# A third of the modulation's dot products, moved from VectorE to GpSimd and ScalarE

## The chip, the cores and the metric

The kernel runs on one core of one Trainium2 chip. The time is the device time of one execution, in microseconds (us). TensorE (PE in the profile) multiplies matrices, VectorE (DVE), ScalarE (ACT) and GpSimd (POOL) work on elements, and SyncE (SP) issues most of the DMAs. Each engine runs its own instructions in order and waits for the others at semaphores.

## The reference, cut to what matters

Two blocks of two layers each run one after the other on 512 rows of 1024 values. Each layer of the first block begins with a modulation, a vector of 6 x 1024 values that shifts, scales and gates the rows of that layer:

```python
c_act = jax.nn.silu(c)                               # 1 x 1024
for layer in range(DEPTH):                           # 2 layers
    mod = c_act @ ada_w[layer] + ada_b[layer]        # 1024 x 6144 weights
    shift1, scale1, gate1, shift2, scale2, gate2 = jnp.split(mod, 6, axis=-1)
    h = modulate(rmsnorm(x, norm1_w[layer]), shift1, scale1)
    ...                                              # layer 0: pooling and attention; layer 1: a state-space mixer
    x = x + gate1[:, None, :] * mix
    h2 = modulate(rmsnorm(x, norm2_w[layer]), shift2, scale2)
    ffn = hier_moe(h2, ...)                          # a router picks 2 of 32 experts for each row
    x = x + gate2[:, None, :] * ffn
```

## The kernel before, in words

Rows lie transposed: a tile holds 128 of the 1024 features on its partitions and the 512 rows along its columns. Every large product is made in three matmuls of split values: a weight tile of 128x1024 is loaded into a stage buffer (`stage`, L286), ScalarE copies its high half (`split`, L278, tile whi), VectorE subtracts to get the low half (L279, tile wlo), and TensorE runs 24 matmuls over it (`mm3`, L304). `proj` does this for one tile of outputs; each call is one step of the program. The stage pool has four buffers, and SP issues the loads in order.

The modulation is not worth a matmul. Its 48 columns per layer (128 values each) are dot products of a transposed weight tile of 128x1024 with the activated vector, which is repeated on all partitions (`cact`, tile row in the profile). One `matvec` loads a tile through the same four stage buffers and lets VectorE multiply and sum it in one instruction (`dot`, L340):

```python
self.nc.vector.scalar_tensor_tensor(t if out is None else out, t, 1.0, vec, op0=OP.mult, op1=OP.mult, accum_out=acc)
```

The first 16 columns of layer 0 are needed at once and are computed ahead of all else (`shift_scale`). The others are pieces of work (`ada_cols`) that `weave` puts into the steps at a rate: 3 to each step of layer 0's mixer, then 1.38 to each step of the state-space mixer. The first list holds columns 16 to 47 of layer 0, then 16 of the second block's modulation, then columns 0 to 15 of layer 1; columns 16 to 47 of layer 1 follow in the state-space mixer. After each eighth column VectorE adds the biases (L407). A scheduler fixes the final order of each engine's instructions from the program.

Around this work stand, in order: layer 0's mixer (projections q, k and u, attention heads in pieces, eight tiles of output weights mix_out), the router of the first mixture of experts (its mask ob is waited for at L839), the experts, the sum of squares (sq on ScalarE, sqa on GpSimd and VectorE in turn, L353 and L355), the normalisation factor rstd as exponential of a logarithm on ScalarE (L367, L368), normalised rows (hhi, L391), and the state-space mixer (weights ssmA), in which GpSimd prepares the tiles aL (L1196). GpSimd's other work in the mixer are running sums for pooling (L612, L613).

Of the kernel before, what the change touches and what calls it, by code (L numbers as in the profile page):

```python
# [15 lines left out]
AF = mybir.ActivationFunctionType  # L16
OP = mybir.AluOpType
# [236 lines left out]
class K:  # L254
# [77 lines left out]
        while q and q[0]:  # L332
            q[0].pop(0)()

    def matvec(self, src, vec, acc):

        self.dot(self.stage(src), vec, acc)

    def dot(self, t, vec, acc, out=None):
        self.nc.vector.scalar_tensor_tensor(t if out is None else out, t, 1.0, vec, op0=OP.mult, op1=OP.mult, accum_out=acc)  # L340
# [58 lines left out]
    def ada_cols(self, l, rng):  # L399

        def one(j):
            def f():
                self.matvec(self.I["adaT"][l, j], self.cact, self.mod[l][:, j:j + 1])
                if j % 8 == 7:
                    a, _ = self.at[f"ada_b{l}"]
                    m = self.mod[l][:, j - 7:j + 1]
                    self.nc.vector.tensor_tensor(m, m, self.cols[:, a + j - 7:a + j + 1], op=OP.add)  # L407
            return f
        return [one(j) for j in rng]
# [1796 lines left out]
```

## Time and profile before

| what | us |
|---|---|
| three executions | 3007.97, 3021.48, 3018.7 |
| their median | 3018.7 |
| profiled execution | 3013.05 |
| its span | 3011.3 |
| TensorE busy | 2827.6 |
| VectorE busy | 1902.1 |
| ScalarE busy | 1254.9 |
| GpSimd busy | 512.4 |

The span goes from the first to the last instruction; what lies around it makes up the profiled execution's time. A row of the profile names the line, engine and operation, the tiles written and read, the count, and the idle time of the engine ahead of it with what ended it.

### The profile page before, as it was taken

How to read it: one execution, taken by the hardware profiler on the slowest of the kernel's cores; microseconds unless marked ns; L12 is line 12 of the kernel's file. 1: busy time of each engine (PE TensorE's matmuls, PEld its weight loads, DVE VectorE, ACT ScalarE, POOL GpSimd, SP SyncE). 2: the span in 40 equal slices, each digit the busy share in tenths (PEclk: the TensorE clock that was granted, in tenths of full speed). 3: DMA queues.
4: the chain of work that ended last, by engine and by line, in shares of the span. 5: the costliest groups of instructions: out<-in, count | busy, mean ns of one | idle time of the engine just before them, and what ended most of it. 6: DMA issues, size and time to landing. Idle time of an engine off the chain costs nothing.

```text
span 3011.3 us, 38668 instructions
## 1 busy us (share of the span) xinstructions
PE 2827.6 (94%) x14382; PEld 2157.5 (72%) x14382; DVE 1902.1 (63%) x3188; ACT 1254.9 (42%) x1989; POOL 512.4 (17%) x451
## 2 busy tenths in 40 slices
PE   7998998799999999887899999999999999999998
PEld 5566855677777786566787677777888767777886
DVE  7787423688889862247789555459547955444444
ACT  3444322455535452246543443343434344333333
POOL 0111321132403232112300100012120000002112
PEclk9999999899999999999999999999999999999999
DMA  8668997555542289974732222237444222222332
GB/s 291 221 224 298 343 412 288 176 176 155 161 143 63 89 309 385 357 262 150 224 111 70 60 77 77 92 113 225 146 139 126 77 63 67 84 91 80 96 91 78
DMA packets 163856, 503.76 MB, mean 167 GB/s; under 512 B 22864, under 2 KB 45008, under 8 KB 151376
## 3 DMA queue, kind: packets, MB, share of 16 engines
q1 hardware_dynamic: 149520, 467.67, 46.5%
q0 software_dynamic: 14144, 33.58, 3.1%
q8 instruction: 114, 1.87, 0.2%
q14 instruction: 78, 0.64, 0.1%
HBM read 472.98 MB, written 46.01 MB: 172 GB/s over the span
## 4 chain that ended last, share of the span: by engine, by line
PE 45%; DVE 4%; issue 1%; ACT 1%; DMA 1%; POOL 0%; DVEq 0%; ACTq 0%; POOLq 0%
PE mm L304 36%; PE po L1492 1%; PE pp L1489 1%; DVE wlo L279 1%; PE po L1415 1%; PE st L1404 1%; PE as L1705 1%; DVE stage L340 1%; PE as L1712 1%; DMA stage<-in_modT_dram 1%; PE pv L1602 0%; PE pv L1601 0%; DVE junk L340 0%; PE po L1426 0%; PE pv L1600 0%
## 5 line engine op out<-in xcount | busy, mean ns | idle before, releaser
L304 PE MATMUL mm<-hhi,whi 128*128 128x512 f32 (+1 forms) x2488 | 932.8, 375 | 11.9 <-ACT hhi L391 4.3
L304 PE MATMUL mm<-hhi,wlo 128*128 128x512 f32 (+1 forms) x2488 | 912.7, 367 | 16.6 <-DVE wlo L279 16.3
L304 PE MATMUL mm<-hlo,whi 128*128 128x512 f32 (+1 forms) x2488 | 909.8, 366 | 0.7 <-POOL hlo L396 0.7
L278 ACT ACTIVATE whi<-stage 128x1024 fp32r<-128x1024 f32 (+2 forms) x477 | 461.5, 968 | 872.2 <-PE mm L304 604.9
L279 DVE TENSOR_TENSOR wlo<-stage,whi 128x1024 fp32r<-128x1024 f32 (+2 forms) x477 | 546.0, 1146 | 425.5 <-issue 193.9
L304 PEld LDWEIGHTS mm<-hhi,whi 128*128 128x128 f32 x2488 | 474.6, 191 | 113.3 <-issue 27.5
L304 PEld LDWEIGHTS mm<-hhi,wlo 128*128 128x128 f32 x2488 | 474.2, 191 | 106.0 <-DVE wlo L279 24.3
L304 PEld LDWEIGHTS mm<-hlo,whi 128*128 128x128 f32 x2488 | 474.6, 191 | 84.9 <-issue 17.6
L340 DVE SCALAR_TENSOR_TENSOR stage<-stage,row 128x1024 f32<-128x1024 f32 x160 | 210.8, 1327 | 24.3 <-DMA stage<-in_adaT_dram 16.6
L1581 POOL TENSOR_TENSOR merged<-sig,merged 128x512 f32<-128x512 f32 x48 | 83.7, 1745 | 559.3 <-DVE sig L1580 550.0
L1617 DVE SCALAR_TENSOR_TENSOR cv<-cfu,cols,cv 128x512 f32<-128x512 f32 x240 | 172.3, 767 | 1.3
L304 PE MATMUL mm<-brh,whi 128*128 128x512 f32 (+1 forms) x384 | 143.0, 373 | 14.0 <-DVE merged L1578 5.8
L304 PE MATMUL mm<-brh,wlo 128*128 128x512 f32 (+1 forms) x384 | 142.3, 374 | 12.7 <-DVE wlo L279 12.4
L304 PE MATMUL mm<-brl,whi 128*128 128x512 f32 (+1 forms) x384 | 139.8, 364 | 0.1
L917 PE MATMUL pa<-w,xc 128*64 128x256 f32 x1056 | 132.4, 391 | 4.1 <-DMA w<-in_w_dram 4.0
L917 PEld LDWEIGHTS pa<-w,xc 128*64 128x64 f32 x1056 | 77.5, 139 | 48.1 <-issue 7.4
L304 PEld LDWEIGHTS mm<-brh,whi 128*128 128x128 f32 x384 | 75.4, 196 | 29.6 <-DVE merged L1578 6.6
L304 PEld LDWEIGHTS mm<-brh,wlo 128*128 128x128 f32 x384 | 75.2, 197 | 27.8 <-DVE wlo L279 16.1
L353 POOL TENSOR_TENSOR sqa<-sq,sqa 128x512 f32<-128x512 f32 (+1 forms) x44 | 58.5, 1329 | 188.8 <-ACT sq L355 183.5
L1356 ACT ACTIVATE att<-as,stat 128x512 f32<-128x512 f32 (+2 forms) x80 | 54.7, 686 | 70.7 <-DVE stat L1467 67.2
L304 PEld LDWEIGHTS mm<-brl,whi 128*128 128x128 f32 x384 | 75.7, 197 | 9.6 <-issue 0.5
L1196 POOL TENSOR_TENSOR aL<-cmt,aah 128x512 fp32r<-128x512 f32 x32 | 51.1, 1598 | 171.1 <-PE pe L1198 143.4
(476 smaller groups left out, 4273.5 us busy)
## 6 DMA issues: line engine op xcount, KB each, us to landing
stage<-in_winA_dram SPq DMA_DIRECT2D x252, 512.0 KB, 3.5
w<-in_w_dram SPq DMA_DIRECT2D x96, 1024.0 KB, 11.7
stage<-in_adaT_dram SPq DMA_DIRECT2D x96, 512.0 KB, 4.5
stage<-in_modT_dram SPq DMA_DIRECT2D x64, 512.0 KB, 3.8
stage<-in_ssmA_dram SPq DMA_DIRECT2D x49, 512.0 KB, 3.5
stage<-in_wbrA_dram SPq DMA_DIRECT2D x96, 256.0 KB, 2.7
stage<-in_woutA_dram SPq DMA_DIRECT2D x24, 512.0 KB, 3.6
dpc<-out SPq DMA_DIRECT2D x41, 256.0 KB, 4.9
```

The costliest lines, as they stand in the source:

```text
L278: self.nc.scalar.activation(hi, src, AF.Copy)
L279: self.nc.vector.tensor_tensor(lo, src, hi.bitcast(FT), op=OP.subtract)
L304: nc.tensor.matmul(ps[:, po:po + n], w[:, k * P:(k + 1) * P], h[:, so:so + n], start=(k == first and w is hi and h is hh), stop=(k == last ...
L340: self.nc.vector.scalar_tensor_tensor(t if out is None else out, t, 1.0, vec, op0=OP.mult, op1=OP.mult, accum_out=acc)
L353: (engine or nc.gpsimd).tensor_tensor(self.sq_acc, self.sq_last, self.sq_acc, op=OP.add)
L917: nc.tensor.matmul(pa[t * C:(t + 1) * C, :256], x[:, k, t * C:(t + 1) * C], w[:, c:c + 256], start=(k == 0), stop=(k == KT - 1))
L1196: nc.gpsimd.tensor_tensor(aL, self.cm("le")[:, None, :].to_broadcast([P, 4, P]), part[:, c, hsl, None].bitcast(FT).to_broadcast([P, 4, P]) ...
L1356: self.nc.scalar.activation(out, in_, func, **kw)
L1404: nc.tensor.matmul(q["ps"][:, i, :T], kT[:, j * P:(j + 1) * P], qT, start=True, stop=True)
L1415: nc.tensor.matmul(q["po"][:, :T], v[j][:, h * P:(h + 1) * P], q[j], start=(j == 0), stop=(j == nt - 1 and cross is None))
L1581: nc.gpsimd.tensor_tensor(merged[f], sg, merged[f], op=OP.add)
L1617: nc.vector.scalar_tensor_tensor(c, u[:, t:t + T], self.col(f"cfw{l}_{t}", i), c, op0=OP.mult, op1=OP.add)
```

## The change

`matvec` gets a flag. With it, GpSimd multiplies the stage tile by the vector in place, and ScalarE copies the product in place and sums it into the column. `ada_cols` sets the flag for columns whose number is a multiple of 3. `ada_cols` makes columns 16 to 47 of layer 0 and all 48 of layer 1, so these are 10 columns of layer 0 (18, 21, ..., 45) and 16 of layer 1 (0, 3, ..., 45), 26 in all; 6 of layer 1's fall into layer 0's mixer. The second block's modulation and `shift_scale` call `matvec` and `dot` without the flag.

```diff
-    def matvec(self, src, vec, acc):
-
-        self.dot(self.stage(src), vec, acc)
+    def matvec(self, src, vec, acc, shared=False):
+
+        t = self.stage(src)
+        if shared:
+            self.nc.gpsimd.tensor_tensor(t, t, vec, op=OP.mult)
+            self.nc.scalar.activation(t, t, AF.Copy, accum_out=acc)
+        else:
+            self.dot(t, vec, acc)
...
-                self.matvec(self.I["adaT"][l, j], self.cact, self.mod[l][:, j:j + 1])
+                self.matvec(self.I["adaT"][l, j], self.cact, self.mod[l][:, j:j + 1], j % 3 == 0)
```

The scheduler then sets other orders on every engine. Lines behind `matvec` move down by 5.

ScalarE at the seam between the first mixture of experts and the state-space mixer; sq are squares of the rows, ms their mean, rstd the normalisation factor. Before:

```order
L355 ACTIVATE sq_4900<-x_157 128x512
L355 ACTIVATE sq_4903<-x_157 128x512
L355 ACTIVATE sq_4906<-x_157 128x512
L372 ACT_TABLE_LOAD
L367 ACTIVATE rstd_4911<-ms_4908,eps 128x512
L368 ACTIVATE rstd_4911<-rstd_4911 128x512
L391 ACTIVATE hhi_4938<-yr_4936,mod_75 128x512
```

and with the change:

```order
L360 ACTIVATE sq_4916<-x_157 128x512
L360 ACTIVATE sq_4919<-x_157 128x512
L360 ACTIVATE sq_4922<-x_157 128x512
L377 ACT_TABLE_LOAD
L372 ACTIVATE rstd_4927<-ms_4924,eps 128x512
L340 ACTIVATE stage_5228,mod_75<-stage_5228 128x1024
L373 ACTIVATE rstd_4927<-rstd_4927 128x512
L396 ACTIVATE hhi_4954<-yr_4952,mod_75 128x512
```

The copy of a shared tile (column 21 of layer 1) now stands between the logarithm and the exponential of rstd.

GpSimd at the same seam; sqa are the running sums of squares, hlo the low halves of the normalised rows. Before:

```order
L353 TENSOR_TENSOR sqa_4886<-sq_4888,sqa_4886 128x512
L353 TENSOR_TENSOR sqa_4886<-sq_4894,sqa_4886 128x512
L353 TENSOR_TENSOR sqa_4886<-sq_4900,sqa_4886 128x512
L396 TENSOR_TENSOR hlo_4945<-yr_4942,hhi_4944 128x512
L396 TENSOR_TENSOR hlo_4958<-yr_4955,hhi_4957 128x512
```

and with the change:

```order
L339 TENSOR_TENSOR stage_5142<-stage_5142,row_161 128x1024
L358 TENSOR_TENSOR sqa_4902<-sq_4904,sqa_4902 128x512
L358 TENSOR_TENSOR sqa_4902<-sq_4910,sqa_4902 128x512
L358 TENSOR_TENSOR sqa_4902<-sq_4916,sqa_4902 128x512
L339 TENSOR_TENSOR stage_5228<-stage_5228,row_161 128x1024
L401 TENSOR_TENSOR hlo_4961<-yr_4958,hhi_4960 128x512
L401 TENSOR_TENSOR hlo_4974<-yr_4971,hhi_4973 128x512
```

One product stands ahead of the first sum, the next one ahead of the low halves.

VectorE in the router, on the way to the mask ob; es, em and ei are steps of the choice of experts. Before:

```order
L810 TENSOR_REDUCE es<-pr 128x32
L814 MAX em<-es 128x8 x3
L815 MAX_INDEX ei<-em,es 128x8 x3
L814 MAX em<-es 128x8
L815 MAX_INDEX ei<-em,es 128x8
L817 TENSOR_TENSOR ex<-em 128x32
```

and with the change:

```order
L815 TENSOR_REDUCE es<-pr 128x32
L279 TENSOR_TENSOR wlo_2577<-stage_2574,whi_2576 128x1024
L819 MAX em<-es 128x8 x3
L820 MAX_INDEX ei<-em,es 128x8 x3
L819 MAX em<-es 128x8
L279 TENSOR_TENSOR wlo_2607<-stage_2604,whi_2606 128x1024
L820 MAX_INDEX ei<-em,es 128x8
L822 TENSOR_TENSOR ex<-em 128x32
```

Two weight subtractions for the context's projections moved into the choice; on TensorE 27 of the context's matmuls, which came behind the mask's matmuls, now come ahead of them.

## Rows read from the trace of the kernel before

**Rows 1.** The page: busy us of each engine; TensorE's busy tenths in 40 slices.

```profile
PE 2827.6 (94%) x14382; PEld 2157.5 (72%) x14382; DVE 1902.1 (63%) x3188; ACT 1254.9 (42%) x1989; POOL 512.4 (17%) x451
...
PE   7998998799999999887899999999999999999998
```

**Rows 2.** Stretches: us; busy us of PE, PEld, DVE, ACT, POOL; granted clock; DMA.

```profile
80.00:100.00 20.00, 14.98 (x40) 7.63 (x41) 12.59 (x34) 10.68 (x18) 6.23 (x8) 0.75 0.56 205
140.00:160.00 20.00, 20.00 (x84) 12.49 (x83) 15.43 (x39) 9.15 (x22) 2.47 (x4) 1.00 0.62 202
560.00:580.00 20.00, 10.62 (x19) 5.60 (x20) 10.51 (x17) 10.14 (x16) 5.68 (x4) 0.59 0.33 107
620.00:640.00 20.00, 20.00 (x109) 15.91 (x110) 16.44 (x28) 11.51 (x14) 9.41 (x7) 1.00 0.53 162
```

**Rows 3.** TensorE's waits from 80 to 300: us in total, times, longest.

```profile
PE sc L645 <- DVE strip L637: 4.2, 2, 3.3
PE pk L839 <- DVE ob L836: 3.8, 1, 3.8
...
PE mm L304 <- DVE wlo L279: 2.1, 3, 0.9
```

**Rows 4.** TensorE's waits from 540 to 740.

```profile
PE ms L363 <- DVE sqa L353: 11.4, 1, 11.4
...
PE pe L1198 <- POOL aL L1196: 1.7, 2, 1.2
```

**Rows 5.** Lines L340 and L279 (80 to 300): duration ns, min/median/max.

```profile
L340 DVE SCALAR_TENSOR_TENSOR stage<-stage,row x160: 1159/1220/2324, 8.9 to 2125.0; 128x1024 f32<-128x1024 f32 x160
L340 DVE DVE_READ_ACCUMULATOR stage<-stage,row x160: 73/82/93, 10.1 to 2126.1; 128x1 f32 x160
...
L279 DVE TENSOR_TENSOR wlo<-stage,whi x26: 1210/1220/1644, 79.3 to 299.5; 128x1024 fp32r<-128x1024 f32 x26
```

**Rows 6.** GpSimd's groups by shape: busy us, mean ns, idle before.

```profile
L353 POOL TENSOR_TENSOR sqa<-sq,sqa 128x512 f32<-128x512 f32 x32 | 46.9, 1465 | 161.5 <-ACT sq L355 156.4 <-DVE sqa L353 4.9
...
L353 POOL TENSOR_TENSOR sqa<-sq,sqa 128x256 f32<-128x256 f32 x12 | 11.6, 966 | 27.4 <-ACT sq L355 27.1
```

**Rows 7.** Lines L278 (90 to 300) and L650 on ScalarE.

```profile
L278 ACT ACTIVATE whi<-stage x26: 1039/1050/1066, 99.3 to 299.4; 128x1024 fp32r<-128x1024 f32 x26
...
L650 ACT ACTIVATION_READ_ACCUMULATOR t<-t,st x32: 185/187/202, 75.9 to 200.8; 128x1 f32 x32
```

**Rows 8.** The seam in order of time: start us, us, engine, line.

```profile
556.63 1.26 POOL L353 TENSOR_TENSOR sqa<-sq,sqa 128x512 f32<-128x512 f32 x1 [20.00 <-ACT sq L355]
...
559.73 2.14 POOL L353 TENSOR_TENSOR sqa<-sq,sqa 128x512 f32<-128x512 f32 x1 [1.84 <-DVE sqa L353]
...
569.54 1.22 DVE L340 SCALAR_TENSOR_TENSOR stage<-stage,row 128x1024 f32<-128x1024 f32 x1 [3.67 <-DMA stage<-in_adaT_dram]
569.69 0.69 ACT L367 ACTIVATE rstd<-ms,eps 128x512 f32<-128x512 f32 x1
570.41 0.63 ACT L368 ACTIVATE rstd<-rstd 128x512 f32<-128x512 f32 x1
...
572.63 0.80 PE L304 MATMUL mm<-hhi,whi 128*128 128x512 f32 x1 [4.26 <-ACT hhi L391]
```

**Rows 9.** VectorE and GpSimd side by side in layer 0's mixer, in order of time.

```profile
182.51 1.15 POOL L612 TENSOR_TENSOR psum<-u 128x511 f32<-128x511 f32 x1
...
182.68 2.06 DVE L340 SCALAR_TENSOR_TENSOR stage<-stage,row 128x1024 f32<-128x1024 f32 x1
183.61 1.18 POOL L613 COPY psum<-u 128x1 f32<-128x1 f32 x1
```

**Rows 10.** SP's stage loads (L286) in layer 0's mixer: first and last start; landing.

```profile
L286 SPq DMA_DIRECT2D stage<-in_mixA_dram x10: 327/328/328, 61.0 to 159.2; - x10
L286 SPq DMA_DIRECT2D stage<-in_mix_out_dram x8: 327/328/340, 170.4 to 237.6; - x8
...
DMA to landing us min/median/max: 3.4/4.5/7.8
```

## The prediction

> **What bounds the kernel now.** I read the page first: TensorE is busy 2827.6 of 3011.3 us, VectorE 1902.1, ScalarE 1254.9, GpSimd 512.4, and TensorE's slices stand at 8 or 9 tenths nearly throughout [rows 1]. So the whole kernel is bounded by TensorE, and a change on the other engines can give back only the places where TensorE waits for them. The 26 products that the change moves lie in two stretches: the first block's mixer and the start of its router (80 to 300 us; 16 products), and the seam from the first mixture of experts to the state-space mixer with the latter's first third (540 to 740 us; 10 products). The table by stretches shows TensorE full in the middle of both (20.00 of 20 us at 140 and at 620) beside a VectorE that is busy 15 to 16 of 20, and two weak places: 14.98 of 20 us at a granted clock of 0.75 at 80, and 10.62 of 20 at 0.59 at the seam at 560 [rows 2]; both clocks are means between the levels of 2.4 and 1.2 GHz, in stretches where TensorE had paused. Then the waits of TensorE by releaser. Of 80 to 300, those on VectorE that the dot products could lengthen are 4.2 us for the strip's memset, 2.1 for the low halves of weights, and 3.8 for the router's mask ob [rows 3]. At the seam one wait of 11.4 us for the sum of squares stands out; GpSimd's aL costs 1.7 [rows 4].
>
> **What is removed.** 26 dot products on VectorE, at a median of 1.220 us and an accumulator read of 0.082 [rows 5]: 26 x 1.30 = 33.9 us of VectorE's time, 20.8 in the first stretch and 13.0 in the second.
>
> **What is added on GpSimd.** 26 multiplications of 128x1024. No row has that shape on this engine. GpSimd's sums take 0.966 us for 256 columns and 1.465 for 512 [rows 6]; each further 256 columns cost 0.499, so 1024 come to 1.465 + 2 x 0.499 = 2.46 us, which I take, since both rows are means over quiet and crowded times alike. Bounds: not under 1.26, the time of a 512-column sum that ran well [rows 8], and not over 2 x 2.14 = 4.28, twice the slow one there [rows 8]. 26 x 2.46 = 64 us on an engine that is busy 17% of the span: it has room.
>
> **What is added on ScalarE.** 26 copies of 128x1024 with a sum: 1.050 us as the weight copies of that shape, and an accumulator read of 0.187 [rows 7]: 1.24 us, 32.2 in all. ScalarE is busy 11.51 of 20 us in the state-space stretch [rows 2], so this and two more loads of its function table, which fall there, are hidden by its idle 8 us; if that cover is gone, the weight copy behind them is late.
>
> **Relief of VectorE.** It is not the whole 33.9 us. A dot product that ran beside GpSimd's sum and copy took 2.06 us, while GpSimd was at work through nearly all of it [rows 9], against 1.22 alone [rows 5]: it went at 0.59 of its speed. If half of VectorE's time under the 64 us of products is of this kind, it loses 64 x 0.5 x 0.41 = 13 us, and 21 are left. The most that this could give is the waits for strip and low halves, 6.3 us [rows 3]. VectorE is busy about 15.4 of 20 us there [rows 2], 170 in 220; an eighth of that goes (20.8), less the loss. I credit a fifth of the waits, -1.3 us. The Trainium skill, page GPSIMD Engine Reference, section Specifications, says that GpSimd shares its SBUF interfaces with VectorE and contends with instructions that have two SBUF inputs; the row agrees. By that rule applied to every product the relief would be about 8 us and the credit 0.5; without contention 34 us and 2.1. So it moves the sum by less than a microsecond either way.
>
> **The router.** VectorE's new order sets two weight subtractions ahead of the mask ob, and TensorE 27 small matmuls of the context into the wait for it. The subtractions cost the chain 2 x 1.22 = 2.44 us [rows 5] of the 3.8 that can be filled [rows 3]. Bounds: a gain of 1.4 or none; I take the middle, -0.7 us.
>
> **The seam.** Here I follow one chain. GpSimd's first sum of squares started at 556.63 [rows 8]; the product now stands ahead of it, but the dot product that stood ahead of VectorE's share of the sums is gone, so I count these as even. Then the next shared tile: its dot product ran at 569.54, after a wait of 3.67 us that ended as the DMA landed [rows 8]. In the new order its ScalarE copy stands between the logarithm (569.69) and the exponential (570.41) of rstd, and the normalised rows that TensorE waits for (4.26 us until 572.63) come behind that [rows 8]. If the tile lands at 569.5 again, GpSimd ends at 572.0 and the copy at 573.2; the exponential is 2.8 us late. Bounds: 1.24 (tile early, the copy alone) to 4.6 (product at 4.28). The tile's issue may come a little earlier, as VectorE is freer: +2.3 us.
>
> **The stage buffers in the mixer.** There are four, and a step takes four tiles: one weight and three vectors. SP issues in order, so a tile that is held blocks the weight behind it. A shared tile lives 4.5 us to landing [rows 10] + 2.46 + 1.24 = 8.2 us, against 4.5 + 1.30 = 5.8 before. A step has (159.2 - 61.0)/9 = 10.9 us in the first part and (237.6 - 170.4)/7 = 9.6 with the output weights [rows 10], so 1.4 us of room are left. With one 512-column sum ahead of it on GpSimd (1.47, [rows 6]) and one weight copy ahead on ScalarE (1.05, [rows 7]) it lives 10.7 and is 1.1 us late. Behind the copy on ScalarE are weight copies and softmax exponentials, which TensorE's order needs. One late step in four of 16: +4.4 us; bounds 0 and 16 x 1.1 = 17.6.
>
> **The state-space third.** Eight products stand among GpSimd's aL, for which TensorE waits 1.7 us now [rows 4]. TensorE has projections to run meanwhile: +1 us; bounds 0 and 8 x 2.46 = 20, were each wait bare.
>
> **Sum.** -1.3 - 0.7 + 2.3 + 4.4 + 1.0 = +5.7 us. Against the profiled execution (span 3011.3, 3013.05 with what lies around it) that is 3018.8. This execution stands 5.7 us below the median of the three runs shown (3018.7); the median of all four is 3015.9, the better base. 3015.9 + 5.7 gives 3021 us: no change that can be told.
>
> **The rivals.**
> *Slower: the held tile.* If GpSimd's product regularly meets another instruction ahead of it, and ScalarE's in-order queue stands behind it, all 16 steps are 1.1 us late: 17.6, with the seam at 4.3, and the other terms as above: +20.9, 3037 us. It decides at the point where a shared tile lives longer than a step, 9.6 us. For it: TensorE is full in these steps [rows 2], so what is late is lost. Against it: the mean step has 1.4 us of room, and GpSimd is idle for most of the stretch (2.47 us busy of 20 at 140, [rows 2]). The Trainium skill, page GPSIMD Engine Reference, section Engine selection, advises against GpSimd for plain elementwise work, as about twice slower than VectorE; 2.46 against 1.22 us agrees, and this rival is how it would cost time here.
> *Faster: VectorE's relief reaches TensorE.* The waits for strip, low halves and mask vanish (4.2 + 2.1 + 3.8), and with them the low clock at 80 us (0.75 over 20 us, so 5.0): 15.1 us, 3001 us. For it: VectorE is the releaser of these waits. Against it: each has other work of VectorE in front of it than the ten shared tiles.
> *No relief.* The products take from VectorE what they free, because most meet two-input instructions: the credit is gone, 3023 us, in measurement the same as the forecast.
>
> **How the numbers follow.** The forecast gets 0.50, the held tile 0.27, no relief 0.14, the faster case 0.09. A measurement of this kernel can tell a difference of about 0.5% (15 us) from no change. The held tile, at 3037, lies beyond that (3033.8) in most of its width; with the forecast's upper tail slower gets 0.27. Faster takes two thirds of its case and a little of the forecast's lower tail, 0.09; same has 0.64. The range goes from 3003, just under the line to faster, to 3042, which is the held tile with some 5 us more for aL; what is left out is about 0.08 below and 0.10 above.
>
> **What would show it.** In the profile after: 26 GpSimd multiplications of about 2.5 us, and 26 copies of 1.05 us with reads; VectorE's busy time down by 20 to 34 us; dot products and subtractions beside products at 1.5 to 2 us. At the seam TensorE's wait for hhi at about 7 us in place of 4.26, with the copy before the exponential. In 80 to 240 us TensorE's waits for whi and wlo should grow by few microseconds: if they grow by over 15, or SP's waits for ScalarE at the stage tiles become long, the held tile was right. I am wrong if TensorE's idle time falls by over 10 us in 80 to 300, or if a GpSimd product takes over 4 us.

## The result, and the profile after

The kernel with the change takes 3050.27 us (median of 6; 3044.99 to 3057.57). The kernel before, run beside it, has a median of 3008.77 (6 runs), and the ratio is 1.0122, 95% interval [1.0106, 1.0138]: about 37 us slower. (The medians of these two sets lie 41.5 us apart: of the six executions before, four took 3008 to 3009 us and two about 3020.) The prediction was 3021 (its sum comes to 3021.6) with a range to 3042, so the time lies above the range, on the side that had a chance of 0.27. The profiled execution took 3051.62 us, its span 3049.8, 38.5 more than before.

The page of the kernel after, for [rows 1]:

```profile
PE 2839.2 (93%) x14382; PEld 2162.3 (71%) x14382; DVE 1898.2 (62%) x3136; ACT 1286.7 (42%) x2043; POOL 578.4 (19%) x477
...
PE   6898997798999999987899999999999999999998
```

GpSimd has 66 us more and ScalarE 32 more, as priced. VectorE, from which 26 dot products were taken (33.9 us), has only 3.9 us less. TensorE is busy 11.6 us longer for the same 14382 matmuls, so some 27 of the 38.5 us are waiting, and the rest is matmuls that took longer. The groups of the new instructions and of the dot products that are left (busy us, mean ns, idle before):

```profile
L345 DVE SCALAR_TENSOR_TENSOR stage<-stage,row 128x1024 f32<-128x1024 f32 x134 | 181.2, 1356 | 37.5 <-DMA stage<-in_adaT_dram 28.7 <-DMA stage<-in_modT_dram 8.4
...
L339 POOL TENSOR_TENSOR stage<-stage,row 128x1024 f32<-128x1024 f32 x26 | 68.0, 2615 | 114.5 <-DMA stage<-in_adaT_dram 61.3 <-DMA dpc<-out 18.7 <-DVE wlo L279 15.9
...
L340 ACT ACTIVATE stage<-stage 128x1024 f32<-128x1024 f32 x26 | 27.5, 1058 | 58.8 <-POOL stage L339 58.8
```

The stretches of [rows 2], whose work now lies somewhat later, so that they show the kind of change and not its sum:

```profile
80.00:100.00 20.00, 15.83 (x45) 8.28 (x46) 11.04 (x30) 11.14 (x19) 10.55 (x10) 0.75 0.44 165
140.00:160.00 20.00, 16.62 (x69) 10.86 (x69) 14.70 (x29) 7.93 (x18) 5.16 (x2) 1.00 0.61 213
560.00:580.00 20.00, 6.77 (x52) 6.29 (x51) 13.01 (x27) 10.28 (x16) 6.94 (x4) 0.78 0.75 237
620.00:640.00 20.00, 15.41 (x64) 11.66 (x63) 16.90 (x27) 11.56 (x19) 10.12 (x7) 0.91 0.52 158
```

The two stretches in which TensorE had been full, 20.00 of 20 us, are full no more: 16.62 and 15.41. In the first of them the granted clock is 1.00 (2.4 GHz) as before, so it is TensorE's waits; in the second it is 0.91, a mean of the levels of 2.4 and 1.2 GHz, where it was 1.00. TensorE's waits of 80 to 300, for [rows 3]:

```profile
PE pp L660 <- DVE t L657: 6.3, 4, 3.7
PE pv L1902 <- ACT whi L278: 4.5, 1, 4.5
PE ms L368 <- ACT sq L360: 3.6, 1, 3.6
PE pp L660 <- DVE st L656: 3.2, 2, 2.9
PE mm L304 <- DVE wlo L279: 3.1, 4, 1.1
```

And those of 540 to 800, for [rows 4]:

```profile
PE ms L368 <- DVE sqa L358: 12.0, 1, 12.0
PE py L1229 <- DVE sg L1210: 7.2, 6, 2.3
PE mm L304 <- ACT hhi L396: 6.5, 1, 6.5
PE py L1229 <- DVE xdt L1219: 3.9, 1, 3.9
PE pe L1203 <- POOL aL L1201: 3.4, 2, 3.0
```

Over the same 260 us before, it waited 2.7 us for sg, 1.7 for aL and not at all for xdt.

**Where the time went.** I compare the start of the n-th matmul into the tiles mm in the two traces and call the difference the lag. It is 0.9 us at 69.7 us (times of the kernel before), 17.7 at 280.8, the end of the mixer, 14.7 at 311, behind the mask, 14.1 at 548, 17.0 at 585.8, behind the seam, 22.0 at 618.9, 33.5 at 781.3 and 36.7 at 835.5; from there to the end it stays between 35.3 and 41.4. So some 17 us are lost in the mixer, 3 are won back in the router, 3 are lost at the seam and 20 in the state-space third. (Of these 20, the last 3 are not clearly the change's: e1 and e5 below, which lose nothing that can be told, gain 1.9 and 2.9 us from 781.3 to 835.5 too.)

**How it is lost** can be read in three places. The first, in the mixer, in order of time:

```profile
119.39 3.19 POOL L339 TENSOR_TENSOR stage<-stage,row 128x1024 f32<-128x1024 f32 x1 [7.36 <-ACT pT L661]
...
120.36 3.30 DVE L345 SCALAR_TENSOR_TENSOR stage<-stage,row 128x1024 f32<-128x1024 f32 x1
...
122.61 1.06 ACT L340 ACTIVATE stage<-stage 128x1024 f32<-128x1024 f32 x1 [2.20 <-POOL stage L339]
...
123.59 0.41 DVE L657 TENSOR_SCALAR t<-t,st 128x384 f32<-128x384 f32 x1
...
124.15 0.53 PE L660 MATMUL pp<-cmt,t 128*128 128x128 f32 x3 [1.09 <-DVE t L657]
```

The product ends at 122.58. The dot product that started beside it takes 3.30 us in place of 1.22 and ends at 123.66, 1.08 behind the product. It has stood still until the product was done, and the softmax piece t, which TensorE waits for, stands behind it. The second place, in the state-space third:

```profile
619.56 2.40 POOL L339 TENSOR_TENSOR stage<-stage,row 128x1024 f32<-128x1024 f32 x1 [15.93 <-DVE wlo L279]
619.58 2.41 DVE L412 TENSOR_TENSOR mod<-mod,cols 128x8 f32<-128x8 f32 x1
...
632.20 2.41 POOL L339 TENSOR_TENSOR stage<-stage,row 128x1024 f32<-128x1024 f32 x1
...
632.31 3.38 DVE L279 TENSOR_TENSOR wlo<-stage,whi 128x1024 fp32r<-128x1024 f32 x1
634.57 2.02 POOL L1201 TENSOR_TENSOR aL<-cmt,aal 128x512 fp32r<-128x512 f32 x1
...
636.64 0.80 PE L1203 MATMUL pe<-aL,gtr 128*128 128x512 f32 x1 [3.04 <-POOL aL L1201]
...
685.41 2.84 DVE L1210 TENSOR_TENSOR sg<-sg,cb 128x512 f32<-128x512 f32 x1 [1.47 <-ACT sg L1205]
```

A sum of 8 columns on VectorE (0.17 us elsewhere) takes as long as the product beside it. At 632 the product stands between two tiles aL, and the second aL then has to stand still itself, beside VectorE's subtraction: TensorE waits 3.04 us. At 685.41 sg starts beside another product (685.35 to 687.71) and takes 2.84 us in place of 0.68; TensorE waits 2.26 us for it. The third place:

```profile
704.03 2.85 POOL L339 TENSOR_TENSOR stage<-stage,row 128x1024 f32<-128x1024 f32 x1
704.54 0.74 DVE L1172 SCALAR_TENSOR_TENSOR acc<-mm,cols,acc 128x510 f32<-128x510 f32 x1
...
706.91 1.06 ACT L340 ACTIVATE stage<-stage 128x1024 f32<-128x1024 f32 x1 [4.04 <-POOL stage L339]
...
708.09 4.99 SPq L286 DMA_DIRECT2D stage<-in_adaT_dram  x2
...
711.49 1.23 DVE L345 SCALAR_TENSOR_TENSOR stage<-stage,row 128x1024 f32<-128x1024 f32 x1 [3.03 <-DMA stage<-in_adaT_dram]
...
714.26 0.72 PE L1229 MATMUL py<-sg,xdt 128*64 128x128 f32 x8 [3.86 <-DVE xdt L1219]
```

Here the sum of the shared tile ends at 708.07, the next load is issued at 708.09, VectorE's dot product waits for its tile until 711.49, 3.4 us later (as long as the shortest load of [rows 10]), and xdt comes behind that and one weight subtraction: the held tile. What such places cost in sum, these rows do not tell; e1 and e18 below bear on it. (The instruction of 704.54, with one input in PSUM, kept its 0.74 us beside the product.)

### The profile page after: what moved, and what is told of

Same layout as the page of the kernel before. It is cut to its first block, busy times and chain, and to the rows that moved or that the text cites. A ratio compares the mean times of both kernels' runs of the same rounds, so it can differ in the third digit from the quotient of the medians.

```text
span 3049.8 us, 38711 instructions
## 1 busy us (share of the span) xinstructions
PE 2839.2 (93%) x14382; PEld 2162.3 (71%) x14382; DVE 1898.2 (62%) x3136; ACT 1286.7 (42%) x2043; POOL 578.4 (19%) x477
## 4 chain that ended last, share of the span: by engine, by line
PE 44%; DVE 4%; issue 1%; DMA 1%; ACT 1%; POOL 0%; DVEq 0%; SPq 0%; ACTq 0%; POOLq 0%
PE mm L304 35%; PE po L1497 1%; DVE wlo L279 1%; PE pp L1494 1%; PE po L1420 1%; PE st L1409 1%; PE as L1710 1%; DMA stage<-in_modT_dram 1%; PE as L1717 1%; PE pv L1606 0%; PE pv L1607 0%; DVE stage L345 0%; PE pv L1605 0%; PE po L1431 0%; PE as L1366 0%
## 5 line engine op out<-in xcount | busy, mean ns | idle before, releaser
L304 PE MATMUL mm<-hhi,wlo 128*128 128x512 f32 (+1 forms) x2488 | 915.9, 368 | 16.5 <-DVE wlo L279 16.1
L278 ACT ACTIVATE whi<-stage 128x1024 fp32r<-128x1024 f32 (+2 forms) x477 | 461.5, 968 | 857.8 <-PE mm L304 585.6
L279 DVE TENSOR_TENSOR wlo<-stage,whi 128x1024 fp32r<-128x1024 f32 (+2 forms) x477 | 550.8, 1157 | 427.6 <-issue 199.0
L345 DVE SCALAR_TENSOR_TENSOR stage<-stage,row 128x1024 f32<-128x1024 f32 x134 | 181.2, 1356 | 37.5 <-DMA stage<-in_adaT_dram 28.7
L1586 POOL TENSOR_TENSOR merged<-sig,merged 128x512 f32<-128x512 f32 x48 | 83.8, 1745 | 558.9 <-DVE sig L1585 549.7
L339 POOL TENSOR_TENSOR stage<-stage,row 128x1024 f32<-128x1024 f32 x26 | 68.0, 2615 | 114.5 <-DMA stage<-in_adaT_dram 61.3
L1361 ACT ACTIVATE att<-as,stat 128x512 f32<-128x512 f32 (+2 forms) x80 | 54.7, 687 | 69.7 <-DVE stat L1472 66.1
```

The source lines that it names most:

```text
L278: self.nc.scalar.activation(hi, src, AF.Copy)
L279: self.nc.vector.tensor_tensor(lo, src, hi.bitcast(FT), op=OP.subtract)
L304: nc.tensor.matmul(ps[:, po:po + n], w[:, k * P:(k + 1) * P], h[:, so:so + n], start=(k == first and w is hi and h is hh), stop=(k == last ...
L339: self.nc.gpsimd.tensor_tensor(t, t, vec, op=OP.mult)
L1361: self.nc.scalar.activation(out, in_, func, **kw)
L1586: nc.gpsimd.tensor_tensor(merged[f], sg, merged[f], op=OP.add)
```

## The experiments

Ratios are to the kernel before, measured beside them; its medians were 3008.8 to 3018.6 us in the different sets, so ratios and not times are compared. (The 37 us above are 0.0122 of 3014.) The theories on record: **L**, VectorE's instructions stand still beside GpSimd's products; **S** or **Q**, the in-order queue of the engine that sums waits for the product; **H**, the stage buffer is held and loads come late. Lags are given at 280.8 (mixer) and at 781.3 (with the seam and most of the state-space third); each is from one profiled execution, and the runs whose ratio cannot be told from 1 (e1, e5, e6, e7, e11, e12, e15) show the chance in them: -2.3 to 3.6 at 280.8, -5.2 to 6.4 at 781.3.

| run | ratio, 95% interval | lag 280.8 | lag 781.3 |
|---|---|---|---|
| the change | 1.0122 [1.0106, 1.0138] | 17.7 | 33.5 |
| e1 product on VectorE | 1.0007 [0.9989, 1.0024] | 3.6 | 3.0 |
| e2 sum on VectorE | 1.0088 [1.0065, 1.0110] | 17.1 | 33.6 |
| e3 mixer only | 1.0048 [1.0033, 1.0062] | 16.0 | 12.3 |
| e4 state-space only | 1.0052 [1.0029, 1.0076] | 0.8 | 26.2 |
| e5 unread product, mixer | 1.0004 [0.9987, 1.0020] | 3.5 | 6.4 |
| e6 unread GpSimd copy, mixer | 0.9988 [0.9973, 1.0002] | 2.5 | 5.2 |
| e7 unread ScalarE copy, mixer | 0.9995 [0.9982, 1.0009] | 0.5 | 2.3 |
| e8 four pieces | 1.0144 [1.0114, 1.0175] | 20.5 | 40.6 |
| e9 unread product on the tile | 1.0112 [1.0089, 1.0135] | 11.9 | 35.7 |
| e10 two products and a reader, mixer | 1.0062 [1.0038, 1.0086] | 18.8 | 20.7 |
| e13 two unread products, mixer | 1.0028 [1.0009, 1.0047] | 12.0 | 11.5 |
| e14 the same in pieces, mixer | 1.0051 [1.0038, 1.0065] | 15.8 | 13.5 |
| e15 ScalarE blocked, mixer | 0.9990 [0.9977, 1.0004] | -1.6 | -5.2 |
| e17 e9 in four pieces | 1.0174 [1.0145, 1.0203] | 21.5 | 47.6 |
| e18 tile held by ScalarE | 1.0047 [1.0033, 1.0061] | 3.8 | 9.6 |

**Which of the two new instructions? (e1, e2)** In e1 the product goes back to VectorE:

```diff
-            self.nc.gpsimd.tensor_tensor(t, t, vec, op=OP.mult)
+            self.nc.vector.tensor_tensor(t, t, vec, op=OP.mult)
```

> The product goes back to VectorE (a tensor_tensor of 128x1024), the sum stays on ScalarE. Theory L (while a GpSimd product runs, a VectorE instruction with two SBUF inputs stands still until it ends, and what TensorE waits for stands behind it): the loss goes with the GpSimd product, 3005 to 3020 us. Theory S (ScalarE's in-order queue stands at the copy, and weight copies and exponentials behind it are late): the copies are still there and still wait for a product, 3035 to 3055 us. Theory H (the stage buffer is held by two engines one after the other, and the loads behind it are late): it is held about 1.2 us shorter than with GpSimd but longer than by one dot product, 3025 to 3040 us.

In e2 VectorE sums instead of ScalarE:

```diff
-            self.nc.scalar.activation(t, t, AF.Copy, accum_out=acc)
+            self.nc.vector.tensor_reduce(acc, t, op=OP.add, axis=mybir.AxisListType.X)
```

> GpSimd keeps the product, VectorE sums it (tensor_reduce, one input), ScalarE gets nothing. Theory L: the products and their locks stay, and VectorE has one more 1.1 us sum for each: 3045 to 3070 us. Theory S: ScalarE's queue is as before, so 3008 to 3022 us. Theory H: the buffer is held as long as in the change, about 3050 us.

Without the GpSimd product nothing is lost; without ScalarE's sum nearly all still is. So the product is the cause. (How it acts e2 does not tell, since VectorE itself now stands 29.1 us at its sums until the products end.) e1 tells more: its tiles are released by ScalarE as in the change, and are held as long. From the issue of a shared tile's load to the end of ScalarE's sum, the change takes 10.1 us on average for the mixer's 16 columns and 8.6 for the other ten, e1 9.8 and 10.0. SP's waits for that from 80 to 300, first in the change, then in e1 (us in total, times, longest):

```profile
SPq L286 <- ACT stage L340: 34.0, 10, 5.4
```

```profile
SPq L286 <- ACT stage L340: 29.5, 11, 5.4
```

Nearly the same holding and nearly the same waits, and no loss. The prediction had named long waits of SP for ScalarE as the sign of the held tile; they are no such sign, since SP waits for some buffer in any case (before, 54.6 us for VectorE's dot products over the same stretch).

**Are the two stretches separate? (e3, e4)** The flag is limited to the mixer's columns (`and (l == 0 or j < 16)`), or to the others (`and l == 1 and j >= 16`).

> Only the 16 columns in layer 0's mixer are shared (not columns 16 to 47 of layer 1). If the losses are local, as the lag of TensorE in the two traces says (about 15 us up to the router, nothing from there to the seam): 3024 us, 3018 to 3030. If the loss is one of the whole order (the scheduler's, or the clock): anything, and the two parts don't add up to the 41.5 us of the change.

> Only the 10 columns at the seam and in the first third of the state-space mixer are shared. If the losses are local: 41.5 less 15 of the mixer, 3034 us, 3027 to 3041, and with the run that shares the mixer's columns alone they add up to 41.5 within 8.

The ratios add up to 1.0100, against 1.0122, which the intervals allow. The lags stand where the products are, so the losses are local. (The profiled execution of e4 was its slowest, 3047 of 3031 to 3047 us, so its 26.2 is high.)

**Small doses in the mixer (e5, e6, e7).** All dot products stay on VectorE; behind 14 columns comes one instruction that nobody reads, in e5

```diff
+            z = self.pjunk.tile([P, 768], BF, tag="junk", name=self.n("junk"))
+            self.nc.gpsimd.tensor_tensor(z, vec[:, :768], acc.to_broadcast([P, 768]), op=OP.mult)
```

in e6 `gpsimd.tensor_copy(z, acc.to_broadcast([P, 768]))`, in e7 `scalar.activation(z, vec[:, :768], AF.Identity, bias=acc)`.

> All dot products stay on VectorE. Behind each of 14 columns in layer 0's mixer GpSimd makes one more product of 128x768 with two SBUF inputs, from the finished column, into a tile that nobody reads; ScalarE gets nothing and no stage buffer is held longer. Theory L: VectorE's two-input instructions that start beside these products end with them plus their own time; without any relief of VectorE, TensorE's lag at the router grows by 6 to 15 us and the ratio to the kernel before is 1.002 to 1.005. Theory H or S (the holding of tiles or ScalarE's queue): 1.000 and a lag under 3 us, since neither is touched.

> As the run with unread products, but GpSimd copies 128x768 (one input, the finished column repeated) instead of multiplying. If the lock of theory L needs two SBUF inputs on GpSimd's side, VectorE's instructions beside the copies keep their usual times, and the ratio is 1.000 with a lag at the router under 3 us. If any GpSimd instruction on SBUF locks VectorE, it is as the run with products (1.002 to 1.005).

> All dot products stay on VectorE and GpSimd gets nothing; ScalarE makes 14 more activations of 128x768 from the finished columns in layer 0's mixer, unread. Theory L: 1.000, a lag at the router under 3 us. Theory S (ScalarE's in-order queue, waiting for a column and busy for about 0.85 us each): 1.002 to 1.005.

e5 missed what I had expected of L. The dose was small: the product with a repeated column takes 1.47 us (median), 23 us in all against the 41.8 of e3, and VectorE's instructions beside them are longer by 6 us in sum, against 23 in e3 (each against the median of its form before). e6 missed too: GpSimd's copies, with one input, also stand still and make stand still (the dot product beside one took 1.83 us, and the copy 1.76 in place of 0.83), but at 0.83 us each they cost nothing measurable.

**Shorter locks (e8).** `for q in range(0, D, D // 4)` around the product, on 256 columns at a time.

> The change, with each product made in four GpSimd instructions of 256 columns. Theory L: VectorE stands still for one piece (about 0.7 us) at a time instead of 2.4 and gets its turn between pieces, so the instructions TensorE waits for are late by less: a ratio of 1.003 to 1.009 in place of the change's 1.0122, and VectorE's excess per locked instruction under 1 us. Theory H or S: the product as a whole takes longer (four starts, and VectorE's turns between), the tile is held and the copy waits longer, 1.012 to 1.018.

It missed L's expectation: not faster than the change (the intervals overlap, so slower is not shown either). VectorE's excess under the products falls from 32 to 19 us, but now its instructions get in between pieces, and the product as a whole takes longer (104 pieces with 96.9 us, against 68.0), with ScalarE waiting 83.8 us for it in place of 58.8.

**The held tile and the reader (e9, e10).** e9 keeps `self.dot(t, vec, acc)` for all columns and adds `self.nc.gpsimd.tensor_tensor(t, t, vec, op=OP.mult)` behind it for the 26. e10 adds to e5's product a second, `gpsimd.tensor_tensor(z, z, vec[:, :768])`, and `scalar.activation(z, z, AF.Copy)` as reader.

> All dot products stay on VectorE, and ScalarE gets nothing. For the same 26 columns GpSimd multiplies the stage tile by the vector once more, in place, behind VectorE's dot product: the product of the change with its shape and inputs, the stage buffer held for it, but no engine that reads it. Theory H (late stage buffers): the buffer is held longer than in the change, so the loss is about as there, 1.010 to 1.016, with a lag of 12 to 20 us at the router. Theory L (VectorE's locked instructions alone): the same number of locks without any relief of VectorE, 1.006 to 1.012, VectorE's excess 15 us or more. Theory Q (an engine that sums stands in its in-order queue at the sum and waits for GpSimd's product, and TensorE's work stands behind it): nobody waits, 0.999 to 1.004, a lag of under 6 us at the router.

> All dot products stay on VectorE and no stage buffer is held longer. Behind 14 columns in layer 0's mixer GpSimd makes two products of 128x768 from the finished column in a tile of its own, and ScalarE copies that tile, unread: it waits for GpSimd as in the change, 14 times about 3 us from the column on. Theory Q: ScalarE's idle time before these copies is 20 us or more and the lag at the router is 8 to 16 us, ratio 1.002 to 1.005. Theory H: nothing is held, as the run with one unread product (a lag of 3.5 us, 1.000). Theory L: a little over that run, as the products are twice as many, 1.001.

e9 costs as much as the change, with no reader at all, so Q is not needed; but VectorE is not relieved and tiles are held. e10 holds no tile and costs 0.6% with half the columns, so H is not needed; but it has both locks and a waiting ScalarE.

**Locks alone, a blocked ScalarE alone (e13, e14, e15).** e13 is e10 without the reader. e14 has its two products in four pieces of 192 columns each. e15 has four ScalarE activations of 128x768 behind each column and no product.

> The run with ScalarE's wait and no held buffer (3035.2 us, 1.0062, a lag of 19 us at the router), without ScalarE's copies: the two GpSimd products of 128x768 behind each of 14 columns stay, and nobody reads them. Theory L: as there, a lag of 12 to 19 us, 1.004 to 1.007. Theory Q: nobody waits, a lag of under 6 us, 0.999 to 1.002.

> The same two unread products, each in four instructions of 192 columns. Theory L: VectorE gets its turn between pieces, and the loss falls with the time that it stands still: if the excess halves, the lag is 6 to 10 us, 1.002 to 1.004. If what counts is GpSimd's busy time as a whole: as the run in whole products.

> All dot products on VectorE, no GpSimd product. Behind each of the 14 columns ScalarE makes four activations of 128x768 in a row, unread: 14 x 4 x 0.93 = 52 us, as long as ScalarE waited in the run with the wait (51.5 us). Theory Q: a lag of 10 to 19 us at the router, 1.003 to 1.006. Theory L: VectorE is untouched, a lag of under 5 us, 0.999 to 1.002.

ScalarE's groups in e15, 60 to 300:

```profile
L343 ACT ACTIVATE junk<-junk,mod 128x768 bf16<-128x768 bf16 x42 | 39.1, 931 | 0.5
...
L341 ACT ACTIVATE junk<-row,mod 128x768 bf16<-128x768 f32 x14 | 13.1, 936 | 11.6 <-DVE stage L346 8.4 <-DVE mod L413 3.1
```

52 us of ScalarE cost nothing: Q alone falls, as far as a queue that is blocked by work stands for one that waits. e13 loses 12 us in the mixer with nothing held and nothing read, a ratio of 1.0028 (a little under L's span). In order of time:

```profile
251.08 1.66 POOL L342 TENSOR_TENSOR junk<-junk,row 128x768 bf16<-128x768 bf16 x1
...
251.12 2.70 DVE L345 SCALAR_TENSOR_TENSOR stage<-stage,row 128x1024 f32<-128x1024 f32 x1
...
252.69 2.24 POOL L358 TENSOR_TENSOR sqa<-sq,sqa 128x512 f32<-128x512 f32 x1
...
253.75 2.27 DVE L279 TENSOR_TENSOR wlo<-stage,whi 128x1024 fp32r<-128x1024 f32 x1
...
256.07 0.79 PE L304 MATMUL mm<-cat,wlo 128*128 128x512 f32 x1 [3.27 <-DVE wlo L279]
```

The engines take turns: the product ends at 252.74, the dot product 1.08 later at 253.82; GpSimd's sum, which waited for it, ends 1.11 later at 254.93; and the subtraction another 1.09 later at 256.02, with TensorE waiting. So it is shown that products which nobody reads and which hold no tile cost time, and here that they do it by turns, theory L. How much of the 12 us comes by turns is not counted: TensorE's waits for wlo from 60 to 300 grow from 2.6 to 8.3 us.

The whole products that nobody reads cost 11.9 (e9) and 12.0 us (e13) in the mixer, those that another engine stands and waits for 16.0 to 18.8 (the change, e2, e3, e10). So a waiting reader may add some 5 us on top of the locks. The lags are single, and in e15 blocks of the same length cost nothing; this stays open.

e14 missed L's expectation as e8 did. VectorE's excess fell only from 19 us (e13) to 15, and its pieces read the columns for longer, and VectorE's bias addition has to wait for that; GpSimd's own sum sqa comes late as well. Its waits of VectorE and of TensorE, 80 to 300:

```profile
DVE mod L414 <- POOL junk L342: 6.6, 2, 5.6
```

```profile
PE mm L304 <- DVE wlo L279: 8.4, 4, 6.0
PE ms L370 <- POOL sqa L360: 6.6, 1, 6.6
```

**What was still open (e17, e18).** e17 is e9 with each product in four pieces. e18 has, in place of e9's product, two copies in place by ScalarE.

> The run with the unread products in place on the stage tile (1.0112), each product in four GpSimd instructions of 256 columns. If the loss goes with the time that one VectorE instruction stands still (at most one piece, about 0.7 us): 1.003 to 1.007. If it goes with GpSimd's busy time as a whole, or with the holding of the tile: 1.010 to 1.016.

> All dot products on VectorE, no GpSimd product; behind each of the 26, ScalarE copies the stage tile in place twice (2 x 1.05 us), unread. Theory H: the buffer is held some 2.1 us and a wait longer, as with the unread product of GpSimd, so 1.007 to 1.013. Theory L: no VectorE instruction stands still, 0.998 to 1.003.

The groups of the unread work in e9, e17 and e18:

```profile
L340 POOL TENSOR_TENSOR stage<-stage,row 128x1024 f32<-128x1024 f32 x26 | 70.0, 2692 | 121.4 <-DVE stage L343 72.6 <-DVE strip L640 12.9 <-issue 12.2
```

```profile
L341 POOL TENSOR_TENSOR stage<-stage,row 128x256 f32<-128x256 f32 x104 | 105.2, 1041 | 123.1 <-DVE stage L344 77.8 <-issue 19.1 <-DVE strip L641 12.4
```

```profile
L341 ACT ACTIVATE stage<-stage 128x1024 f32<-128x1024 f32 x52 | 54.8, 1054 | 27.8 <-DVE stage L344 21.9 <-DVE pl L623 2.8 <-DVE Ac L1876 2.7
```

Pieces are worse again (1.0174 against 1.0112), now without a bias addition in the way. So the loss does not go with the time that a single VectorE instruction stands still, but rather with how long GpSimd's work takes as a whole: 105.2 us in pieces, 70.0 in one. One place in the mixer of e17 shows how:

```profile
263.11 5.72 POOL L341 TENSOR_TENSOR stage<-stage,row 128x256 f32<-128x256 f32 x4 [3.83 <-DVE stage L344]
268.80 1.26 POOL L357 TENSOR_TENSOR sqa<-sq,sqa 128x512 f32<-128x512 f32 x1
...
270.11 1.22 PE L367 MATMUL ms<-sqa,cmt 128*128 128x512 f32 x1 [5.71 <-POOL sqa L357]
```

The first piece takes 0.74 us. Each of the other three meets one of VectorE's dot products and takes 1.70, so the four take 5.72 where a whole product takes 2.34 alone. GpSimd's sum stands behind them in GpSimd's own queue, and TensorE waits 5.71 us for it, against 0.6 in e9; e14 has the same wait (6.6 us above), e13 none. So turns cost GpSimd's own work too, a rival to L that no run was made for: in the change TensorE's waits for sqa of GpSimd are 0.3 us in the mixer, those for aL 3.4 in the state-space third.

e18 costs 1.0047 without GpSimd: 3.8 us of lag in the mixer, little more than chance, and 9.6 by 781.3. Its tiles are held for 10.4 us in the mixer and 11.9 behind it, in the latter longer than in the change; and it gives ScalarE 54.8 us more, which e15 showed to be harmless in the mixer alone. Which of the two costs is not told apart.

**A version that beats both (e11, e12, e16).** These are edits of the kernel before. e11 lets TensorE sum the squares at the seam, e12 puts the sums of squares behind the experts on VectorE alone, e16 all sums of squares and all low halves of normalised rows:

```diff
-                (engine or nc.gpsimd).tensor_tensor(self.sq_acc, self.sq_last, self.sq_acc, op=OP.add)
+                nc.vector.tensor_tensor(self.sq_acc, self.sq_last, self.sq_acc, op=OP.add)
...
-            if k % 2 == 0:
+            if True:
                 nc.vector.scalar_tensor_tensor(lo, y, Bc[:, k:k + 1], hi.bitcast(FT), op0=OP.add, op1=OP.subtract)
```

> The kernel before, with the sum of squares at the seam made by TensorE: each of the eight squares goes through the matrix of ones into one accumulator as it comes, in place of seven sums by GpSimd and VectorE in turn and two matmuls. By the rows of before the squares start at 555.4 and a matmul takes 1.03, so the last ends near 564.3 in place of 568.4: 4 us less, and up to 8 if TensorE's clock stays up. Ratio 0.997 to 0.999. Rival: what is won is waited for behind the seam (loads, rstd): 1.000.

> The kernel before, with all sums of squares behind the mixtures of experts on VectorE (three chains of seven sums; four of each seven were on GpSimd). Theory L reads the sums of 1.26 to 2.14 us there as locks between GpSimd and VectorE's dot products; on VectorE alone a chain takes 7 x 0.69 = 4.8 us and one or two dot products of 1.3 between, against 8.1 us: about 1 to 2 us less at each of the three places, 0.998 to 1.000. Rival: VectorE's dot products get in between more of the sums: 1.000 to 1.002.

> The kernel before, with GpSimd's 44 sums of squares and 28 low halves of normalised rows on VectorE (the low halves without ScalarE's second pass). Theory L: the 25 us by which these lengthen VectorE's instructions in the kernel before go, VectorE gains some 30 + 21 us of work in their place, and at the seams, where TensorE waits, the chain is shorter by 1 to 3 us each: 0.995 to 0.999. Rival: VectorE's added work is late for TensorE in the full stretches, 1.000 to 1.004.

e11: 0.9996 [0.9981, 1.0011], e12: 0.9989 [0.9975, 1.0004], neither told from no change. e16: 3004.01 us (median of 7, 2997.62 to 3010.53) against 3017.5, 0.9952 [0.9935, 0.9968], some 14 us faster than the kernel before. Its page:

```profile
PE 2830.5 (94%) x14382; PEld 2154.8 (72%) x14382; DVE 1919.1 (64%) x3260; ACT 1238.4 (41%) x1961; POOL 419.8 (14%) x379
```

GpSimd gives up 92.6 us, and VectorE takes over 72 instructions for only 17.0 us more. ScalarE has 16.5 us less as well, since 28 second passes over normalised rows go with the edit, so that the gain is not shown to be GpSimd's alone. Where the 14 us are won its profile does not show: that execution took 3010.53 us, the slowest of the seven, and its wait at the seam is no shorter (12.5 us for sqa, before 11.4 [rows 4]).

## Why the prediction was wrong

**The relief of VectorE (forecast -1.3).** The step that failed first. I had seen the right rows and misread them. The dot product of 2.06 us [rows 9] I took for one that ran at 0.59 of its speed, so that half of VectorE's time under the products would cost 13 us. It is a lock: the sum on GpSimd ended at 182.51 + 1.15 = 183.66, the dot product at 184.74, 1.08 later, as at 123.66 above. The third line of the same rows says it too: GpSimd's copy of one column took 1.18 us, where the shortest of that line takes 0.18, and ended just behind the dot product. Read so, every such instruction that starts beside a product loses what is left of it, however small it is. Measured under the 26 products: 32 us longer in sum, against 33.9 removed. VectorE got nearly nothing (3.9 us less busy, where 20 to 34 were forecast), and the small instructions that TensorE waits for came up to 2.3 us late. The Trainium skill, page SBUF — State Buffer, section SBUF: two separate sides, says just this: of a VectorE instruction with two SBUF inputs and a GpSimd instruction that reads SBUF, whichever starts first keeps the shared pair for its whole length, and the other waits fully. The traces agree, both ways round (the subtraction of 632.31 and the aL of 634.57). The prediction had used only that the two contend.

**The product (2.46 us).** Its size was right: median 2.40, shortest 2.34, mean 2.62, since a product that starts beside a VectorE instruction waits for that first (3.19 at 119.39). ScalarE's copy, 1.058 and 0.186, was right.

**The router (-0.7).** The lag falls by 3.0 there, from 17.7 to 14.7; the order moved as I said, and TensorE's wait for the mask, 3.8 us [rows 3], is gone. It goes with the order, as the prediction had it, and not with the product: it is gone in e1, e7 and e15 too, in which two weight subtractions also stand ahead of ob, and is 3.8 again in e9 and e13, in which none does. Mis-sized by 2.3, beyond its bound.

**The seam (+2.3).** Right by its steps. In the profile after:

```profile
586.46 1.06 ACT L340 ACTIVATE stage<-stage 128x1024 f32<-128x1024 f32 x1 [1.21 <-POOL stage L339]
...
587.51 0.61 ACT L373 ACTIVATE rstd<-rstd 128x512 f32<-128x512 f32 x1
...
589.72 0.79 PE L304 MATMUL mm<-hhi,whi 128*128 128x512 f32 x1 [6.48 <-ACT hhi L396]
```

The copy stands before the exponential, and the wait is 6.48 in place of 4.26 us [rows 8], 2.2 more; the sums of squares, counted as even, cost 0.6.

**The mixer (+4.4 for the stage buffers).** Measured about 17. The lag is near the 17.6 of the rival of the held tile, but that is luck, and not its mechanism alone: holding without GpSimd gave a lag of 3.8 there, little more than chance (e18), tiles held as long in e1 (9.8 us against 10.1) cost nothing that can be told, and products without a held tile cost 12 (e13). The rival's sign did not come either: from 80 to 240 TensorE's waits for whi and wlo did not grow by 15 us, they fell from 2.6 to 1.5. Its price for the whole kernel, 3037, was also too low.

**The state-space third (+1).** The term that missed by most: about 20, the upper bound that I had given and set aside because TensorE had projections to run meanwhile. It had, but its waits are for single instructions of the chain (sg 7.2 us, xdt 3.9, aL 3.4), and at the places shown above they come behind a lock, a product or a late tile. Besides, from 585.8 to 781.3 the same matmuls kept TensorE busy 5.2 us longer, at a granted clock of 0.98 where it was 1.00; the prediction had no term for that. How the 20 us divide among lock, product and late tile was not settled: products without a held tile were not tried there. Against the late tile speaks e1, which held its tiles there for 10.0 us, longer than the change, and had a lag of 3.0 at 781.3; for it e18, with up to 9.6.

**What stays open** besides: how much of the loss is VectorE's standing still and how much is GpSimd's own work that comes late in its queue, and whether a waiting reader adds to both. That the products on GpSimd make the loss is shown (e1, e9, e13), and that the two engines take turns; that the loss is in proportion to the time VectorE stands still is not, and e14 and e17 speak against it: VectorE's excess was lower there (15 us against 19, 22 against 38), and the time was no better.

## What to carry to other kernels

Before work moves from VectorE to GpSimd, look for a VectorE instruction in the trace that lasts as long as the GpSimd one beside it: then the two take turns, the moved work relieves nobody, and small instructions on the path to TensorE come late by a whole GpSimd instruction. Test the parts of such a change apart (product here, sum there); one run each told that the loss goes with GpSimd's product and not with ScalarE's sum. The other direction can pay: taking short two-input work away from GpSimd, and a pass of ScalarE with it, made this kernel 0.5% faster at 17 us more on VectorE.

## What was not expected of the hardware

A sum of 8 columns took 2.41 us beside a product, as against 0.17. GpSimd's copy with a single input took part in the turns as well (e6: 0.83 us alone, 1.76 beside a dot product). An instruction of VectorE with an input in PSUM kept its 0.74 us. And the shorter pieces, meant to soften the turns, made no kernel faster; in e17 they made it slower beyond the intervals.
